# A second projection whose products are added up in PSUM: TensorE keeps adding into banks that have already been read

## The chip, the core and the metric

The kernel runs on one core of one Trainium2 chip. A core has five engines with a queue each: TensorE (matrix products, results only into PSUM), VectorE, ScalarE, GpSimd and SyncE, which here only starts transfers. PSUM has eight banks of 512 fp32 values per partition; one product of this kernel fills one bank. The time is that of the whole program on the device, in microseconds. Beside the timed runs there is one profiled execution, from which the profile and the trace come.

## The reference: what is computed

One layer of an encoder for 2048 tokens of width 1024 in fp32: windowed attention, then a SwiGLU feed-forward network with 2816 hidden units, each followed by a normed, gated residual:

```python
h = rmsnorm(x, ffn_norm_pre[i]) * (1.0 + sc2) + sh2
y = swiglu(h, ffn_w_in[i], ffn_w_out[i])       # (silu(a) * b) @ w_out
x = x + g2 * rmsnorm(y, ffn_norm_post[i])
```

The change lies in `@ w_out` (the second projection: 2816 values in, 1024 out) and in the norm and residual after it.

## The kernel before, in words

*How fp32 is kept.* Every fp32 factor is split into a high half, rounded to the matmul's input type by ScalarE, and a low half, the rest, by VectorE (`split`, L149 to L151). A product of two 128-wide tiles is then three matmuls: high by high, high by low, low by high.

*How the projection is tiled.* The tokens are done in two halves of 1024, each half as two chunks of 512. The output's 1024 columns are two groups of 512. So a half's result is a 2 x 2 block matrix (column group i, chunk j), and the 2816 hidden values are 11 pairs of 128-wide tiles. For each pair the 2 x 2 by 2 x 2 block product is done with seven products in place of eight, by Winograd's form of Strassen's method. The factors are sums of blocks: s1 to s4 of the weights, made by GpSimd (L1147, L1148, L1166, L1168), and t1 to t4 of the hidden values, made earlier and kept in DRAM (`g_d`). With P1 = a11 b11, P2 = a12 b21, P3 = s4 b22, P4 = a22 t4, P5 = s1 t1, P6 = s2 t2, P7 = s3 t3, the four results are

```
(0,0) = P1 + P2          (0,1) = P1 + P6 + P5 + P3
(1,0) = P1 + P6 + P7 + P4    (1,1) = P1 + P6 + P7 + P5
```

*How it is staged.* `PARTS` (L55) groups the pairs: parts of 2, 3, 3, 3 pairs in the first half and 3, 3, 3, 2 in the second; the last one (`LAST`) is done as eight plain products a block (`plain`, L1217). A stage is one of the seven products of one part, for the four 128-token blocks of a chunk in turn. `product` (L1196) takes a bank of the pool `psO` (six banks, used in rotation), adds the matmuls of the part's pairs in it (9 for three pairs), and empties it into an SBUF tile of its own for each product and block: in a half's first part ScalarE copies it (L1207), later VectorE adds it (L1209). So 7 x 4 running sums are kept. In the half's last such part the combinations above are made in SBUF from the seven sums (`SUMS`, L1109, at L1213; those into "2" and "3" by VectorE, the others by GpSimd).

*What comes with it.* `Weights.put` splits the weights of one stage, three stages ahead, and loads a part's raw weights into the buffers `raw0` to `raw2` as soon as their last use is over. `Grams.load` fetches the hidden factors two stages ahead into twelve buffers; for the first half it also splits them, for the second they lie in DRAM as halves. The first stages' factors are prepared while the first projection ends (`first_weights`, L987).

*The norm.* `finish` (L1233) handles one block and chunk: it loads the residual x1, squares the two result tiles with ScalarE, multiplies them by the gains with VectorE (L1245), forms the reciprocal root of the mean, scales, adds the residual (L1249) and stores. `ahead` (L1253) strings eight of these for the first half; one step of it is issued after every product of the second half's first part.

*The order.* Within an engine, instructions run in the order in which the program's planner has put them. It goes by program order as priority and by simulated times, so a changed instruction can move its neighbours.

Of the kernel before, what the change touches and what calls it, by code (L numbers as in the profile page):

```python
# [17 lines left out]
P = 128  # L18
# [49 lines left out]
def encoder_layer(ctx, tc, a):  # L68
# [361 lines left out]
    psF = open_pool(ctx, "psF", 2, space=PSUM)  # L430
# [136 lines left out]
    def make_row(col, dst, scratch, i):  # L567
        pg = psF.tile([P, CH], F32, tag="mm", name=f"pgrow{i}")
# [200 lines left out]
    def filling():  # L769
# [14 lines left out]
        make_row(coef[:, 1, :], g1row, yq.tile([P, CH], F32, tag="sq", name="growt0", bufs=1), 0)  # L784
# [202 lines left out]
    def first_weights():  # L987
# [14 lines left out]
        for i in range(2):  # L1002
            for k in range(m):
                t = b21p.tile([P, 2, CH], F32R, tag="b21", name=f"g0_{i}_{k}")
                sp.dma_start(f(t[:, 1]), g_d[0][k][("t1", "b21")[i]][:, 0])
# [3 lines left out]
        for i, n in enumerate(("s1", "a12", "a11")):  # L1009
            for k, src in enumerate(first_src):  # L1010
# [5 lines left out]
                elif n == "a12":  # L1016
                    pool.tensor_tensor(src["s4"], src["a12"], src["s2"], ALU.subtract)
# [70 lines left out]
    for hf in range(S // HALF):  # L1088
# [8 lines left out]
        if hf + 1 < S // HALF:  # L1097
# [3 lines left out]
    psc.close()  # L1101

# [8 lines left out]
    AGAIN = dict(zip("5216473", "1678924"))  # L1111
    PLACE = {(0, 0): "2", (0, 1): "3", (1, 0): "4", (1, 1): "5"}
# [9 lines left out]
    psO = open_pool(ctx, "psO", 6, space=PSUM)  # L1122
# [7 lines left out]
    class Weights:  # L1130
# [20 lines left out]
        def put(self, n=1):  # L1151
            for _ in range(n):
# [7 lines left out]
                for k, src in enumerate(self.src):  # L1160
# [6 lines left out]
                    elif name == "a12" and (hf, p) != LAST:  # L1167
# [27 lines left out]

    def product(hf, p, i, b):  # L1196
        m, name = PARTS[hf][p], PRODUCTS[i][2]
        ps = psO.tile([P, CH], F32, tag="p", name=f"po{hf}_{p}_{i}_{b}")
        for k in range(m):
            g, w = grams.g[hf, p, i, k][:, :, b * P:(b + 1) * P], wts.w[hf, p, i, k]  # L1200
            pe.matmul(ps, g[:, 0], w[:, 0], start=k == 0, stop=False)  # L1201
            pe.matmul(ps, g[:, 0], w[:, 1], start=False, stop=False)  # L1202
            pe.matmul(ps, g[:, 1], w[:, 0], start=False, stop=k == m - 1)  # L1203
        if p == 0:
            slot = AGAIN[name] if hf else name
            z[hf, b, name] = (zB if slot in "37" else zC if slot in "89" else zA).tile([P, CH], F32, tag=f"z{slot}", name=f"z{hf}_{b}_{name}", bufs=JB)
            act.copy(z[hf, b, name], ps)  # L1207
        else:
            dve.tensor_tensor(z[hf, b, name], ps, z[hf, b, name], ALU.add)  # L1209
        if (hf, p) in ((0, len(PARTS[0]) - 1), (1, len(PARTS[1]) - 2)):  # L1210
            for x, *y in SUMS.get(name, ()):
                y = [x] + y if len(y) == 1 else y
                (dve if x in "23" else pool).tensor_tensor(z[hf, b, x], z[hf, b, y[0]], z[hf, b, y[1]], ALU.add)  # L1213
# [3 lines left out]
    def plain(j, b):  # L1217

        hf, p = LAST
        for i in range(2):  # L1220
            ps = psO.tile([P, CH], F32, tag="p", name=f"pl{j}_{b}_{i}")
# [8 lines left out]
            y = z[hf, b, PLACE[i, j]]  # L1230
            dve.tensor_tensor(y, ps, y, ALU.add)

    def finish(hf, j, b):  # L1233
# [7 lines left out]
        ys = [z[hf, b, PLACE[i, j]] for i in range(2)]  # L1241
# [28 lines left out]
    end = iter(())  # L1270
    for hf, p in parts[:-1]:
        for i in range(len(PRODUCTS)):
            for b in range(JB):
                product(hf, p, i, b)
                next(end, None)
            wts.put()
            grams.load()
        if (hf, p) == (0, 0):
            with tc.issue_after(latest[0]):
                make_row(coef[:, 3, :], grow, yp.tile([P, CH], F32, tag="sq", name="growt1", bufs=2), 1)  # L1280
        if (hf, p) == (0, len(PARTS[0]) - 1):
            end = ahead([finish(hf, j, b) for b in range(JB) for j in range(CPH)])
# [66 lines left out]
```

## Time and profile before

| | |
|---|---|
| time, median of 3 runs | 2104.68 us (2103.5 to 2110.62) |
| profiled execution: its time, its span | 2106.09 us, 2104.3 us |
| TensorE busy | 2019.6 us, 96% of the span |
| VectorE, ScalarE, GpSimd busy | 1528.5, 1005.2, 969.4 us |
| second projection, first product to end of the plain part | 1654.4 to 2095.2 us of the span |

In the trace, `po` is the bank of a product, `z` the running sums, `wo_s` and `wo_a` split weights of a sum or a plain block, `wr` raw weights, `g` hidden factors. A window's row gives each engine's busy time and, in brackets, its instructions. Matmuls overlap: each is listed for about 0.39 us, though they start 0.227 us apart. A half is written 0 or 1 and a part by its number, so the second half's first part is part (1,0).

### The profile page before, as it was taken

The numbers are of one execution on the slowest core, as the hardware profiler recorded it, in microseconds if no ns is written. First come the engines' busy times: TensorE is split into PE (matmuls) and PEld (weight loads), VectorE is DVE, ScalarE is ACT, GpSimd is POOL, SyncE is SP. The second block draws the span as 40 slices with busy tenths as digits, with TensorE's granted clock in tenths as the row PEclk, the third lists the DMA queues.
The fourth block names the chain that finished last, engine by engine and source line by source line (L and its number), as shares of the span: only waits on it lengthen the run. The fifth ranks groups of instructions, "written<-read, shape, count | busy, mean of one in ns | idle before, by whom it ended". The sixth has DMA issues, their size and how long they took to land.

```text
span 2104.3 us, 28775 instructions
## 1 busy us (share of the span) xinstructions
PE 2019.6 (96%) x9416; PEld 1663.9 (79%) x9416; DVE 1528.5 (73%) x2621; ACT 1005.2 (48%) x2129; POOL 969.4 (46%) x934
## 2 busy tenths in 40 slices
PE   8797899999999998999999999999999999999998
PEld 6676787888888786888888887888888788877886
DVE  8376677667777668576676698777875689987667
ACT  4233577776777756333333344434333654435222
POOL 0412446543445535455665455555453242395340
PEclk9899999999999999999999999999999999999999
DMA  8689668565555675443743454534434454469763
GB/s 313 189 281 284 185 184 263 175 166 182 168 187 202 212 241 187 140 129 118 247 158 108 160 177 151 196 140 178 162 145 160 151 196 135 135 249 365 264 243 128
DMA packets 257286, 402.69 MB, mean 191 GB/s; under 512 B 84661, under 2 KB 135397, under 8 KB 255088
## 3 DMA queue, kind: packets, MB, share of 16 engines
q1 hardware_dynamic: 216592, 371.41, 52.3%
q10 hardware_dynamic: 39072, 25.18, 3.9%
q0 software_dynamic: 1472, 4.27, 0.5%
q8 instruction: 74, 1.21, 0.2%
q14 instruction: 76, 0.62, 0.1%
HBM read 267.83 MB, written 132.95 MB: 190 GB/s over the span
## 4 chain that ended last, share of the span: by engine, by line
PE 72%; DVE 10%; DMA 7%; POOL 4%; issue 3%; ACT 3%; SPq 0%; DVEq 0%; ACTq 0%; POOLq 0%
PE pc_i L147 12%; PE pc_i L145 12%; PE pc_i L146 12%; PE po L1202 4%; PE po L1203 4%; PE po L1201 4%; PE t L519 3%; PE psq L146 2%; PE psq L147 2%; PE psq L145 2%; PE s L497 2%; PE py L613 2%; PE py L614 2%; PE py L615 2%; PE o L525 2%
## 5 line engine op out<-in xcount | busy, mean ns | idle before, releaser
L146 PE MATMUL pc_i<-ht,ws_i 128*128 128x512 f32 x528 | 207.5, 393 | 1.6 <-DVE ht L151 1.6
L145 PE MATMUL pc_i<-ht,ws_i 128*128 128x512 f32 x528 | 206.5, 392 | 1.6 <-ACT ht L150 1.6
L147 PE MATMUL pc_i<-ht,ws_i 128*128 128x512 f32 x528 | 207.4, 393 | 0.0
L150 ACT CAST wa_i<-wiri 128x512 fp32r<-128x512 f32 x132 | 81.7, 620 | 212.6 <-PE pc_i L147 121.6
L506 POOL TENSOR_SCALAR pr<-pr,rs 128x288 f32<-128x288 f32 (+3 forms) x256 | 125.4, 509 | 117.7 <-DVE rs L504 108.0
L502 ACT ACTIVATE pr<-pr,nm 128x289 f32<-128x289 f32 (+3 forms) x256 | 135.3, 530 | 58.5 <-DVE nm L500 57.0
L500 DVE CUSTOM_DVE_ANT_0 pr<-s,bias,nsink 128x288 f32<-128x288 f32 (+3 forms) x256 | 124.0, 500 | 53.4 <-PE s L497 41.9
L878 POOL TENSOR_TENSOR s_i<-wiri 128x512 f32<-128x512 f32 x44 | 61.3, 1394 | 193.1 <-DMA wiri<-w_in 146.1
L151 DVE TENSOR_TENSOR ws_i<-s_i,ws_i 128x512 fp32r<-128x512 f32 x132 | 126.7, 960 | 24.1 <-ACT ws_i L150 23.9
L151 DVE TENSOR_TENSOR wa_i<-wiri,wa_i 128x512 fp32r<-128x512 f32 x132 | 125.2, 948 | 20.2 <-ACT wa_i L150 19.7
L145 PE MATMUL pc_i<-hb,wa_i 128*128 128x512 f32 x352 | 139.0, 395 | 0.5 <-DVE u_i L945 0.5
L151 DVE TENSOR_TENSOR plo<-t,phi 128x512 fp32r<-128x512 f32 x184 | 121.8, 683 | 24.1 <-ACT phi L150 24.0
L146 PE MATMUL pc_i<-hb,wa_i 128*128 128x512 f32 x352 | 138.2, 393 | 0.0
L147 PE MATMUL pc_i<-hb,wa_i 128*128 128x512 f32 x352 | 138.2, 393 | 0.0
L1201 PE MATMUL po<-wo_s,g 128*128 128x512 f32 x320 | 125.2, 395 | 5.9 <-ACT wo_s L150 5.3
L1202 PE MATMUL po<-wo_s,g 128*128 128x512 f32 x320 | 126.0, 394 | 1.8 <-DVE wo_s L151 1.8
L497 PE MATMUL s<-k,q 128*128 128x288 f32 (+4 forms) x512 | 110.4, 314 | 17.1 <-DMA k<-k_d 11.0
L1203 PE MATMUL po<-wo_s,g 128*128 128x512 f32 x320 | 125.7, 393 | 0.0
L519 PE MATMUL t<-ident,pr 128*128 128x128 f32 x736 | 116.2, 275 | 6.6 <-POOL pr L506 5.8
L146 PEld LDWEIGHTS pc_i<-ht,ws_i 128*128 128x128 f32 x528 | 99.7, 189 | 23.9 <-DVE ht L151 2.1
L145 PEld LDWEIGHTS pc_i<-ht,ws_i 128*128 128x128 f32 x528 | 99.9, 189 | 23.5 <-ACT ht L150 2.0
L150 ACT CAST ws_i<-s_i 128x512 fp32r<-128x512 f32 x132 | 81.6, 618 | 75.7 <-PE pc_i L147 71.1
(253 smaller groups left out, 6037.5 us busy)
## 6 DMA issues: line engine op xcount, KB each, us to landing
wiri<-w_in SPq DMA_DIRECT2D x88, 512.0 KB, 4.0
ada<-ada_w SPq DMA_DIRECT2D x40, 512.0 KB, 6.7
wr<-w_out SPq DMA_DIRECT2D x20, 1024.0 KB, 9.1
g<-g_d_t SPq DMA_DIRECT2D x36, 512.0 KB, 5.6
g<-g_d_b SPq DMA_DIRECT2D x35, 512.0 KB, 5.3
q<-q_d SPq DMA_DIRECT2D x16, 1024.0 KB, 6.6
wsr<-w_qkv SPq DMA_DIRECT2D x24, 512.0 KB, 4.9
g<-g_d_t SPq DMA_DIRECT2D x44, 256.0 KB, 3.2
```

The lines of the kernel that those rows point to most:

```text
L145: pe.matmul(ps, w[0], h[0], start=first, stop=False)
L146: pe.matmul(ps, w[0], h[1], start=False, stop=False)
L147: pe.matmul(ps, w[1], h[0], start=False, stop=last)
L150: act.copy(hi, src)
L151: return eng.tensor_tensor(lo, src, f(hi), ALU.subtract).ins
L497: m = pe.matmul(ps[:, :n], qs, kk[:, e, jb * P + lo:jb * P + hi], start=e == 0, stop=e == 1)
L502: act.activation(pr[:, i, lo:hi + 1], pr[:, i, lo:hi + 1], AF.Exp, bias=nm[:, i:i + 1], scale=-1.0, accum_out=rs[:, i:i + 1])
L506: pool.tensor_scalar(pr[:, i, lo:hi], pr[:, i, lo:hi], rs[:, i:i + 1], 1.0, ALU.mult, ALU.mult)
L519: pe.transpose(pt[:, i * P:(i + 1) * P], pr[:, i, jj * P:(jj + 1) * P], ident)
L1201: pe.matmul(ps, g[:, 0], w[:, 0], start=k == 0, stop=False)
L1202: pe.matmul(ps, g[:, 0], w[:, 1], start=False, stop=False)
L1203: pe.matmul(ps, g[:, 1], w[:, 0], start=False, stop=k == m - 1)
```

## The change

`PRODUCTS` gets a new order, and in place of a sum's name each product has a tag and a place. The tag names a set of four banks, one for each block: a or b. The first three products start their bank afresh (`FRESH`); the other four add their matmuls to what their bank already holds, after it has been read once: set a goes from P1 to P1 + P6, P1 + P6 + P7 and P1 + P6 + P7 + P4, set b from P5 to P5 + P3. After each product the bank's content of that time is added to the result at its place (or copied there, if it is the first for that place). Four results for each block are kept in SBUF, and `SUMS` with its additions is gone. The pool `psO` has eight banks, four in each set, where it had six; the two come from the pool `psF`, which now closes before. A part begins with a12 in place of s1, and s4 is made together with s2. The row of gains (`make_row`) takes a bank of set a. The norm of the first half begins one stage earlier, goes through the blocks of the first chunk before the second's, and takes a step after every second product. `first_weights` follows the new order.

```diff
-    PRODUCTS = (("s1", "t1", "5"), ("a12", "b21", "2"), ("a11", "b11", "1"), ("s2", "t2", "6"),
-                ("a22", "t4", "4"), ("s3", "t3", "7"), ("s4", "b22", "3"))
+    psf.close()
+    PRODUCTS = (("a12", "b21", "a", (0, 0)), ("s1", "t1", "b", (1, 1)), ("a11", "b11", "a", (0, 0)), ("s2", "t2", "a", (0, 1)),
+                ("s3", "t3", "a", (1, 1)), ("a22", "t4", "a", (1, 0)), ("s4", "b22", "b", (0, 1)))
+    FRESH = 3
-    SUMS = {"1": (("2", "1"),), "6": (("6", "1"), ("1", "6", "5")), "7": (("7", "6"), ("4", "7"), ("5", "7")),
-            "3": (("3", "1"),)}
...
-    psO = open_pool(ctx, "psO", 6, space=PSUM)
+    psO = open_pool(ctx, "psO", JB, space=PSUM)
...
                     if name == "s1":
                         pool.tensor_tensor(src["s2"], src["s1"], src["a11"], ALU.subtract)
-                    elif name == "a12" and (hf, p) != LAST:
                         pool.tensor_tensor(src["s4"], src["a12"], src["s2"], ALU.subtract)
...
+    bank = {}
     def product(hf, p, i, b):
-        m, name = PARTS[hf][p], PRODUCTS[i][2]
-        ps = psO.tile([P, CH], F32, tag="p", name=f"po{hf}_{p}_{i}_{b}")
+        m = PARTS[hf][p]
+        _, _, tag, at = PRODUCTS[i]
+        if i < FRESH:
+            bank[tag, b] = psO.tile([P, CH], F32, tag=tag, name=f"po{hf}_{p}_{i}_{b}")
+        ps = bank[tag, b]
         for k in range(m):
             g, w = grams.g[hf, p, i, k][:, :, b * P:(b + 1) * P], wts.w[hf, p, i, k]
-            pe.matmul(ps, g[:, 0], w[:, 0], start=k == 0, stop=False)
...
+            on = dict(skip_group_check=True) if i >= FRESH else {}
+            pe.matmul(ps, g[:, 0], w[:, 0], start=i < FRESH and k == 0, stop=False, **on)
...
-        if p == 0:
-            slot = AGAIN[name] if hf else name
-            z[hf, b, name] = (zB if slot in "37" else zC if slot in "89" else zA).tile([P, CH], F32, tag=f"z{slot}", name=f"z{hf}_{b}_{name}", bufs=JB)
-            act.copy(z[hf, b, name], ps)
+        if (hf, b, at) in z:
+            y = z[hf, b, at]
+            dve.tensor_tensor(y, ps, y, ALU.add)
         else:
-            dve.tensor_tensor(z[hf, b, name], ps, z[hf, b, name], ALU.add)
-        if (hf, p) in ((0, len(PARTS[0]) - 1), (1, len(PARTS[1]) - 2)):
-            for x, *y in SUMS.get(name, ()):
-                y = [x] + y if len(y) == 1 else y
-                (dve if x in "23" else pool).tensor_tensor(z[hf, b, x], z[hf, b, y[0]], z[hf, b, y[1]], ALU.add)
+            pl = (zC if at[0] else zB) if hf else zA
+            y = z[hf, b, at] = pl.tile([P, CH], F32, tag=f"z{at[0]}{at[1]}", name=f"z{hf}_{b}_{at[0]}{at[1]}", bufs=JB)
+            act.copy(y, ps)
...
-    end = iter(())
+    end, turn = iter(()), 0
     for hf, p in parts[:-1]:
         for i in range(len(PRODUCTS)):
+            if (hf, p, i) == (0, len(PARTS[0]) - 1, len(PRODUCTS) - 1):
+                end = ahead([finish(0, j, b) for j in range(CPH) for b in range(JB)])
             for b in range(JB):
                 product(hf, p, i, b)
-                next(end, None)
+                turn += 1
+                if turn % 2 == 0:
+                    next(end, None)
             wts.put()
             grams.load()
         if (hf, p) == (0, 0):
             with tc.issue_after(latest[0]):
-                make_row(coef[:, 3, :], grow, yp.tile([P, CH], F32, tag="sq", name="growt1", bufs=2), 1)
-        if (hf, p) == (0, len(PARTS[0]) - 1):
-            end = ahead([finish(hf, j, b) for b in range(JB) for j in range(CPH)])
+                make_row(coef[:, 3, :], grow, yp.tile([P, CH], F32, tag="sq", name="growt1", bufs=2), 1,
+                         psO.tile([P, CH], F32, tag="a", name="pgrow1"))
```

More of the change, by code (lines that the diff above doesn't have):

```diff
@@ L429, in encoder_layer @@
     ada_late = open_pool(com, "adal", 2)
-    psF = open_pool(ctx, "psF", 2, space=PSUM)
+    psf = ExitStack()
+    psF = open_pool(psf, "psF", 2, space=PSUM)
     psS = open_pool(att, "psS", 2, space=PSUM)
@@ L565, in fill_qkv, with make_row @@
                         nxt.halves(k)
-    def make_row(col, dst, scratch, i):
-        pg = psF.tile([P, CH], F32, tag="mm", name=f"pgrow{i}")
+    def make_row(col, dst, scratch, i, pg):
         pe.transpose(pg[:KT, :P], col, ident)
@@ L783, in filling @@
         g1row = yq.tile([P, D], F32, name="g1row")
-        make_row(coef[:, 1, :], g1row, yq.tile([P, CH], F32, tag="sq", name="growt0", bufs=1), 0)
+        make_row(coef[:, 1, :], g1row, yq.tile([P, CH], F32, tag="sq", name="growt0", bufs=1), 0,
+                 psF.tile([P, CH], F32, tag="mm", name="pgrow0"))
         yield from fillers_o()
@@ L1004, in first_weights @@
                 t = b21p.tile([P, 2, CH], F32R, tag="b21", name=f"g0_{i}_{k}")
-                sp.dma_start(f(t[:, 1]), g_d[0][k][("t1", "b21")[i]][:, 0])
+                sp.dma_start(f(t[:, 1]), g_d[0][k][("b21", "t1")[i]][:, 0])
                 split(t[:, 0], t[:, 1], f(t[:, 1]), dve)
@@ L1008, in first_weights @@
         yield
-        for i, n in enumerate(("s1", "a12", "a11")):
+        for i, n in enumerate(("a12", "s1", "a11")):
             for k, src in enumerate(first_src):
@@ L1015, in first_weights @@
                     pool.tensor_tensor(src["s2"], src["s1"], src["a11"], ALU.subtract)
-                elif n == "a12":
                     pool.tensor_tensor(src["s4"], src["a12"], src["s2"], ALU.subtract)
@@ L1194, in encoder_layer @@
     z = {}
+    bank = {}
     def product(hf, p, i, b):
[L1197 to L1198 removed]
+        m = PARTS[hf][p]
[3 more added lines that the diff above has]
+        ps = bank[tag, b]
         for k in range(m):
             g, w = grams.g[hf, p, i, k][:, :, b * P:(b + 1) * P], wts.w[hf, p, i, k]
[L1201 to L1213 removed]
+            on = dict(skip_group_check=True) if i >= FRESH else {}
+            pe.matmul(ps, g[:, 0], w[:, 0], start=i < FRESH and k == 0, stop=False, **on)
+            pe.matmul(ps, g[:, 0], w[:, 1], start=False, stop=False, **on)
+            pe.matmul(ps, g[:, 1], w[:, 0], start=False, stop=k == m - 1, **on)
+        if (hf, b, at) in z:
+            y = z[hf, b, at]
+            dve.tensor_tensor(y, ps, y, ALU.add)
+        else:
+            pl = (zC if at[0] else zB) if hf else zA
+            y = z[hf, b, at] = pl.tile([P, CH], F32, tag=f"z{at[0]}{at[1]}", name=f"z{hf}_{b}_{at[0]}{at[1]}", bufs=JB)
+            act.copy(y, ps)
     grow = zB.tile([P, D], F32, name="grow")
@@ L1220, in plain @@
         for i in range(2):
-            ps = psO.tile([P, CH], F32, tag="p", name=f"pl{j}_{b}_{i}")
+            ps = psO.tile([P, CH], F32, tag="ab"[i], name=f"pl{j}_{b}_{i}")
             m = PARTS[hf][p]
@@ L1229, in plain @@
                     pe.matmul(ps, g[:, 1], w[:, 0], start=False, stop=k == m - 1 and e == 1)
-            y = z[hf, b, PLACE[i, j]]
+            y = z[hf, b, (i, j)]
             dve.tensor_tensor(y, ps, y, ALU.add)
@@ L1240, in finish @@
         ss = yp.tile([P, 2], F32, tag="ss", name=f"ss{c}_{b}", bufs=3)
-        ys = [z[hf, b, PLACE[i, j]] for i in range(2)]
+        ys = [z[hf, b, (i, j)] for i in range(2)]
         for i in range(2):
```

2 lines of the change are left out of this document (removed).

## The prediction

> **What bounds the kernel now.** I read the page, then windows cut at the parts of the second projection, then windows of its tile `po` alone, then the chain of waits at the places that lose time. First the page:
>
> ```profile
> span 2104.3 us, 28775 instructions
> PE 2019.6 (96%) x9416; PEld 1663.9 (79%) x9416; DVE 1528.5 (73%) x2621; ACT 1005.2 (48%) x2129; POOL 969.4 (46%) x934
> ```
>
> TensorE is the bound, and the diff issues the same matmuls in the same number. It can therefore win only time in which TensorE waits inside the second projection, and it can lose there. One window for each part, the plain part and the tail:
>
> ```profile
> core 0: us, PE busy (x) PEld busy (x) DVE busy (x) ACT busy (x) POOL busy (x), PEclk, DMA share, GB/s
> 1654.44:1697.46 43.02, 40.43 (x170) 32.72 (x169) 27.19 (x35) 35.67 (x67) 13.52 (x10) 0.96 0.69 243
> 1697.46:1756.22 58.76, 57.42 (x253) 47.22 (x252) 53.97 (x68) 27.22 (x48) 25.74 (x17) 1.00 0.43 144
> 1756.22:1813.34 57.12, 57.12 (x253) 47.30 (x252) 50.88 (x71) 25.22 (x43) 18.34 (x12) 1.00 0.46 152
> 1813.34:1870.46 57.12, 57.12 (x253) 47.30 (x252) 49.29 (x72) 20.94 (x36) 27.92 (x19) 1.00 0.62 213
> 1870.46:1932.18 61.72, 58.61 (x253) 46.91 (x252) 53.27 (x89) 32.87 (x88) 41.79 (x37) 1.00 0.74 290
> 1932.18:1994.52 62.34, 59.14 (x254) 48.20 (x252) 41.54 (x52) 16.93 (x29) 25.00 (x18) 0.97 0.76 285
> 1994.52:2051.64 57.12, 57.12 (x254) 47.30 (x252) 39.41 (x56) 11.95 (x20) 24.70 (x17) 1.00 0.68 249
> 2051.64:2095.20 43.56, 43.56 (x193) 35.85 (x191) 34.65 (x74) 13.49 (x44) 5.01 (x4) 1.00 0.39 132
> 2095.20:2104.31 9.11, 0.12 (x1) 0.00 (x0) 4.37 (x10) 1.13 (x4) 0.00 (x0) 0.69 0.31 115
> ```
>
> A part of three pairs has 7 x 4 x 9 = 252 matmuls and takes 57.12 us where nothing waits: 0.2267 us a matmul, 2.04 a product, 8.16 a stage of four products. The first part has two pairs, so 57.12 x 2/3 = 38.08 (a stage 5.44). The losses are 43.02 - 38.08 = 4.94, then 1.64, 4.60 (the fifth window) and 5.22 (the sixth): 16.40 us in all. That is the most that can be won; the plain part loses nothing, and the diff only renames tiles in the tail. Which stages lose it, and one that does not (same columns, without GpSimd):
>
> ```profile
> 1665.73:1673.94 8.21, 5.62 (x25) 4.32 (x23) 0.00 (x0) 2.25 (x4) 1.00 0.72 245
> 1673.94:1681.14 7.20, 7.20 (x24) 5.79 (x25) 0.00 (x0) 1.54 (x3) 0.76 0.06 22
> 1697.46:1707.26 9.80, 8.46 (x37) 6.68 (x36) 0.00 (x0) 1.82 (x3) 1.00 0.20 58
> 1731.74:1739.90 8.16, 8.16 (x37) 6.76 (x36) 1.37 (x2) 0.00 (x0) 1.00 0.75 269
> 1886.78:1898.29 11.51, 8.92 (x37) 6.41 (x35) 0.00 (x0) 2.28 (x4) 1.00 0.07 12
> 1898.29:1907.38 9.09, 8.59 (x36) 6.79 (x37) 0.00 (x0) 3.10 (x6) 1.00 0.99 380
> 1932.18:1945.56 13.38, 10.18 (x38) 7.65 (x36) 1.97 (x3) 2.26 (x4) 0.87 0.98 385
> ```
>
> First part: 8.21 - 5.44 = 2.77 of waiting, then 1.76 at a clock of 0.76. Then 1.64 at the second part's first stage; 3.35 + 0.93 in the second half's first part; 5.22 at the first stage of the part after. What ended the first and the last of these, from the chain of waits:
>
> ```profile
> 1670.78 0.62 ACT g L150
> 1671.40 0.97 ACT z L1207 x2
> 1672.37 0.38 ACT g L150
> 1672.78 0.59 ACT z L1207
> 1673.37 0.53 ACT wo_s L150
> ...
> 1916.77 18.15 DMA wr<-w_out
> ...
> 1936.42 0.64 ACT wo_s L150
> 1937.08 1.42 DVE wo_s L151
> ```
>
> And in between, from the waits of 1870 to 1946 us, and SyncE's own:
>
> ```profile
> PEld po L1201 <- ACT z L1207: 5.2, 5, 3.0
> ACT sq L1244 <- POOL z L1213: 7.2, 1, 7.2
> ...
> SPq L1238 <- DVE z L1249: 22.1, 3, 17.7
> ```
>
> TensorE waited there for banks that ScalarE had not emptied, and ScalarE stood behind squares of the norm that waited for GpSimd's sums.
>
> **The change part by part.** Prices of one eviction and of the sums:
>
> ```profile
> L1209 DVE TENSOR_TENSOR z<-po,z x140: 674/685/694, 1709.0 to 2052.5; 128x512 f32<-128x512 f32 x140
> L1207 ACT COPY z<-po x56: 563/587/615, 1657.4 to 1938.5; 128x512 f32<-128x512 f32 x56
> ```
> ```profile
> L1213 POOL TENSOR_TENSOR z<-z,z 128x512 f32<-128x512 f32 x38 | 60.1, 1606 | 67.8 <-DVE z L1209 67.5
> L1213 DVE TENSOR_TENSOR z<-z,z 128x512 f32<-128x512 f32 x15 | 13.5, 900 | 0.6
> ```
>
> Evictions stay at 7 x 4 x 7 = 196, so accumulating saves none of them. Copies fall from 56 to 32 and adds rise from 140 to 164: ScalarE -24 x 0.587 = -14.1 us, VectorE +24 x 0.685 = +16.4. The sums go: -60.1 us on GpSimd, -13.5 on VectorE. VectorE's total moves by +3, which nothing waits for as such; what counts is where.
>
> *First part (4.53 of its 4.94).* The copies of stage two leave ScalarE: 0.97 + 0.59 = 1.56 us of the chain above. VectorE must add them instead before stage three enters the same banks, 4 x 0.685 = 2.74 in the worst order, so between 1.2 worse and 4.53 better. In that window ScalarE is the fuller engine (35.67 against 27.19 us of 43.02). I take the copies' 1.5 as **won**.
>
> *Second part's first stage (1.64).* Each part now begins with a12, which needs no GpSimd sum, where s1 did. But VectorE has eight more adds before it (5.5 us). Between 0 and 1.64; I take **1.0**.
>
> *Norm of the first half (4.60).* The sums that the squares waited for are gone, and the steps come every second product: 17 steps over 34 products, 69 us, not 35. Against it VectorE, 53.27 us busy in this window of 61.72, gets 12 adds (8.2 us) and loses the sums there and a sixth of the norm. Its loads and stores are as many, eight loads on SyncE, sixteen stores from GpSimd; a load that waits for its buffer (22.1 us above) still has gram loads queued behind it, which are fetched two stages, 16 us, ahead. I take the stall as gone but for 1.0: **3.6**, from -4.1 (a rival below) to 4.60. The Trainium skill ("SBUF — State Buffer", "Who interferes with whom") says that a VectorE instruction with two SBUF inputs contends with a GpSimd one that reads SBUF, and one with a single SBUF input does not. The trace agrees: at most 694 ns for the add from PSUM, 900 on average for L1213 beside GpSimd. By that rule the 1.0 would be gone too, and the sum 1.0 us better.
>
> *Part after it (5.22).* The weights' last tile took 18.15 us to land, among stores and loads of the norm at 385 GB/s, and was issued late behind the norm's VectorE work. Then s1 was summed, cast and split: from 1934.92 (1916.77 + 18.15) to the cast at 1936.42 is 1.5 us that a12 spares in any case. With the norm spread the transfer should start and land earlier. Between 1.5 and 5.22, I take **4.2**.
>
> *The banks.* Six rotating banks gave a bank five products until its next use. Now stages two to five of a part add into the same four banks, so an eviction has three products, 6.1 us. VectorE's queue in two stages where weights and grams are split, with GpSimd busy:
>
> ```profile
> 1731.94 0.69 DVE L1209 TENSOR_TENSOR z<-po,z 128x512 f32<-128x512 f32 x1
> ...
> 1735.93 0.68 DVE L1209 TENSOR_TENSOR z<-po,z 128x512 f32<-128x512 f32 x1
> ...
> 1739.34 3.47 DVE L151 TENSOR_TENSOR g<-g 128x512 fp32r<-128x512 f32 x2
> 1742.73 1.27 DVE L1209 TENSOR_TENSOR z<-po,z 128x512 f32<-128x512 f32 x2
> ...
> 1752.34 1.28 DVE L1209 TENSOR_TENSOR z<-po,z 128x512 f32<-128x512 f32 x2
> ...
> 1799.76 1.28 DVE L1209 TENSOR_TENSOR z<-po,z 128x512 f32<-128x512 f32 x2
> ```
>
> The stage began at 1731.74; the add at 1731.94 is still the last of the stage before, 1735.93 its own first, and the pair at 1742.73 its second and third. The second is done at 1743.42, but its bank is wanted at 1739.90 + 2.04 = 1741.94: 1.5 us of waiting. One part later the stage begins 57.12 us on, at 1788.86; the add is done at 1800.45 and wanted at 1799.06: 1.4. The third such part shows no late pair. Cost **-2.9**; 0 if the order falls well. If the later pair at 1752.34 (done 1753.03, wanted one stage after 1741.94, at 1750.10) stood in a chained stage, 2.9 in each of three parts, -8.8. A wait this short costs no clock: the 1.64 above ran at 1.00.
>
> The row of gains now borrows one of these banks, once, for a transpose and a small copy. Seven products lie between its turn and the next use of that bank, so I cost it at nothing; with that cover gone TensorE waits for a copy, at most L1207's 0.59.
>
> Sum: 1.5 + 1.0 + 3.6 + 4.2 - 2.9 = **7.4 us**. The span goes from 2104.3 to 2096.9. The profiled execution took 2106.09, 1.8 around its span and 1.4 above the median shown, so I take the change from the median: 2104.68 - 7.4 = **2097.3**.
>
> **The rivals.** *All stalls go* and the late pairs come out early: 16.4 won, 2088.3. For it: every loss has a cause that the diff touches. Against: the pairs are late by GpSimd's weight sums, which stay.
>
> *The gain is eaten.* The first two places stay as they are, the transfer of 18.15 us still ends last and only the 1.5 of the sum goes, the norm gives 3.6, the banks take 2.9: 2.2 won, 2102.5. For it: DMA at 385 GB/s, with the same bytes to move.
>
> *The norm's backlog meets fewer banks: slower.* In the second half's first part evictions and norm stand in the same queues. If they stay as late as now, a bank that has three products in place of five waits 2 x 2.04 = 4.1 us more than the 4.60 of today; with 2.9 in the first half and nothing won elsewhere that is +7.0, 2111.7. It decides where an eviction lags over 6.1 us. For it: VectorE at 86% gets 12 more adds. Against: no sums, half the pace. The Trainium skill ("Perfetto Trace Analysis", "Matmuls") speaks for this one: matmul groups should rotate through different banks so that one's evacuation overlaps the next. No run yet shows its price here.
>
> **How the numbers follow.** Forecast 0.48, all stalls go 0.12, eaten 0.25, slower 0.15. About 0.3%, 6.3 us, is what a measurement tells from no change: faster 0.60, same 0.25, slower 0.15. The range leaves out the outer half of the two ends: 2089 to 2108.
>
> **What would show it.** Right: part windows after of some 41.5, 59.3, 58.5, 57.1, 58.1, 58.1 and 57.1 us; no GpSimd or VectorE instruction on the sums' line; TensorE's waits for an eviction on VectorE of 1 to 2 us in the middle stages of two first-half parts; the weight transfers of the second half's second part landing before their stage. Wrong: a second half's first part over 61.7 us with TensorE waiting for adds (the slower rival), the first stage after it still waiting for `wr`, or first-half parts longer than 60 us.

## The result, and the profile after

The changed kernel takes 2089.72 us (median of 4 runs, 2086.54 to 2092.54); the kernel before, beside it, 2105.21 us. The ratio is 0.9921 with a 95% interval of 0.9901 to 0.9941: 15.5 us less. Forecast were 7.4 us less, 2097.3. The time lies in the range; the change of it is twice the forecast. A second measurement of both, below, gives 0.9945 (0.9926 to 0.9965), 11.4 us by the medians (2102.67 over 23 runs of the kernel before, 2091.29 over 7 of the changed one).

The first lines of the page of the changed kernel:

```profile
span 2084.7 us, 28731 instructions
PE 2011.4 (96%) x9416; PEld 1660.3 (80%) x9416; DVE 1505.5 (72%) x2629; ACT 994.7 (48%) x2105; POOL 912.5 (44%) x894
```

TensorE issues 9416 matmuls as before. GpSimd has 40 instructions less, ScalarE 24 less, VectorE 8 more. Windows of the changed kernel, one for each part, then the plain part (columns as in the prediction):

```profile
1645.58:1688.26 42.68, 41.16 (x170) 32.58 (x168) 31.48 (x46) 29.96 (x55) 13.45 (x10) 0.96 0.65 227
1688.26:1745.51 57.25, 57.25 (x255) 47.32 (x254) 54.89 (x72) 27.16 (x47) 26.20 (x17) 1.00 0.46 157
1745.51:1802.62 57.11, 57.11 (x253) 47.31 (x252) 50.42 (x71) 25.74 (x43) 18.73 (x12) 1.00 0.46 153
1802.62:1859.74 57.12, 57.12 (x253) 47.31 (x252) 48.69 (x72) 25.21 (x54) 18.14 (x12) 1.00 0.65 230
1859.74:1917.81 58.07, 57.46 (x253) 47.23 (x252) 48.43 (x92) 28.20 (x65) 25.20 (x28) 1.00 0.94 354
1917.81:1974.93 57.12, 57.12 (x253) 47.31 (x252) 36.91 (x50) 12.85 (x22) 18.69 (x13) 1.00 0.68 248
1974.93:2032.05 57.12, 57.12 (x253) 47.31 (x252) 32.15 (x49) 11.95 (x20) 0.00 (x0) 1.00 0.69 252
2032.05:2075.60 43.55, 43.55 (x193) 35.86 (x191) 32.35 (x72) 13.50 (x44) 0.00 (x0) 1.00 0.38 128
```

Four parts now run at 57.12 us, the time without a wait, and two others at 57.25 and 58.07. Against the windows of the kernel before, part (0,1) is 1.51 us shorter, (1,0) 3.65, (1,1) 5.22, the first part 0.34. From the first product to the end of the plain part it is 430.16 us where it was 440.88: 10.7 us less.

The rest of the difference between the two profiles lies before the change: the projection's first product starts at 1645.58 us, where it started at 1654.44, 8.9 us earlier. Up to the last stages of the first projection the two kernels have the same instructions in the same order on every engine. Fourteen profiles of this study start the projection between 1645.3 and 1654.4 us, two of them of the unchanged kernel, at 1654.4 and 1649.6. The kernel before and its variants (four profiles) start it at 1647.4 to 1654.4, the changed kernel and its variants (ten) at 1645.3 to 1652.3. So the start scatters by several microseconds by itself, and the reading below goes by the projection's own length.

Table of all profiles, from the starts of the `po` matmuls in the trace (us). The parts (0,2), (0,3) and (1,2) are 57.12 in all of them, but for 58.26 and 57.22 in the first two of "s1 first". The columns are the parts, the projection's length to the end of the plain part, and the projection's start.

| kernel | (0,0) | (0,1) | (1,0) | (1,1) | length | start |
|---|---|---|---|---|---|---|
| before | 43.0 | 58.8 | 61.7 | 62.3 | 440.9 | 1654.4 |
| before, again | 40.6 | 61.7 | 63.6 | 61.4 | 442.3 | 1649.6 |
| after | 42.7 | 57.3 | 58.1 | 57.1 | 430.2 | 1645.6 |
| after, again | 41.1 | 57.3 | 57.6 | 57.1 | 428.1 | 1648.5 |
| before, a12 first | 40.4 | 57.1 | 65.0 | 58.3 | 435.9 | 1647.4 |
| after, s1 first | 41.1 | 62.2 | 57.4 | 57.1 | 434.1 | 1650.2 |
| after, old pace | 41.1 | 57.3 | 57.8 | 57.1 | 428.2 | 1647.0 |
| after, sums back | 41.1 | 58.2 | 77.6 | 57.1 | 449.0 | 1651.0 |
| after, sums and pace back | 42.7 | 57.3 | 76.6 | 57.1 | 448.7 | 1652.3 |
| after, sums that only the norm waits for | 41.2 | 57.4 | 64.9 | 60.1 | 438.6 | 1648.2 |
| after, VectorE made late | 41.1 | 58.1 | 58.0 | 64.7 | 436.9 | 1647.8 |
| before, VectorE made late | 43.1 | 58.9 | 62.8 | 65.3 | 445.2 | 1648.6 |
| after, s2 earlier | 39.0 | 58.8 | 57.7 | 57.1 | 427.6 | 1645.3 |
| after, s2 earlier, look-ahead kept | 38.7 | 58.9 | 58.0 | 57.1 | 427.8 | 1649.1 |

Below, the *lag* of an eviction is the time from the end of its product's last matmul to its own end, and the *cover* of a bank is how long the lag may be before TensorE, which wants the bank again, has to wait.

### The profile page after: what moved, and what is told of

Read it like the earlier page. It is cut to its first block, busy times and chain, and to the rows that moved or that the text cites. A ratio compares the mean times of both kernels' runs of the same rounds, so it can differ in the third digit from the quotient of the medians.

```text
span 2084.7 us, 28731 instructions
## 1 busy us (share of the span) xinstructions
PE 2011.4 (96%) x9416; PEld 1660.3 (80%) x9416; DVE 1505.5 (72%) x2629; ACT 994.7 (48%) x2105; POOL 912.5 (44%) x894
## 4 chain that ended last, share of the span: by engine, by line
PE 42%; DVE 4%; DMA 1%; issue 1%; POOL 1%; ACT 1%; SPq 0%; DVEq 0%; ACTq 0%; POOLq 0%
PE pc_i L145 8%; PE pc_i L147 8%; PE pc_i L146 8%; PE po L1205 5%; PE po L1206 5%; PE po L1204 5%; DVE z L1245 1%; PE pl L1229 1%; PE pl L1227 1%; PE pl L1228 1%; DMA wiri<-w_in 0%; DVE z L1249 0%; DMA ht<-hd_d_t 0%; DVE z L1209 0%; DVE wo_s L151 0%
## 5 line engine op out<-in xcount | busy, mean ns | idle before, releaser
L1209 DVE TENSOR_TENSOR z<-po,z 128x512 f32<-128x512 f32 x164 | 110.6, 684 | 42.2 <-PE po L1206 40.4
L498 PE MATMUL s<-k,q 128*128 128x288 f32 (+4 forms) x512 | 110.0, 313 | 16.7 <-DMA k<-k_d 10.4
```

## The experiments

### Both kernels once more

No edit. The unchanged kernel against itself:

> The kernel before once more. Theory scatter: projection 440.8 us (within 1.5), its start anywhere from 1645 to 1655. Rival, upstream is part of the change: the start again at 1653 to 1656. Either: no difference in time from before.

> The changed kernel once more. Its first profile has 8.9 us of the difference ahead of the projection (first product at 1645.6 us, 1654.4 before), where both kernels issue the same instructions, and 10.7 us in it (first product to the last of the plain part: 430.0 us, 440.8 before). Theory scatter: the start of the projection varies from execution to execution whatever the kernel, so it lies anywhere from 1645 to 1655 here, and the projection again takes 430 us (within 1). Rival, upstream is part of the change: the start is again 1645 to 1647.

Measured: the unchanged kernel 2103.23 us, ratio to itself 1.0006 (0.9986 to 1.0026); the changed one 2091.29 us, ratio 0.9945 (0.9926 to 0.9965). What follows: the gain is there again, in the same three parts. The two starts, 1649.6 and 1648.5 us, are 1.1 apart, not 8.9, which speaks for scatter and against the rival. The changed kernel's projection is 2 us shorter than in its first profile (428.1), more than the 1 us expected, most of it (1.6) in the first part. The whole program's gain is 15.5 us in one measurement and 11.4 in the other; the projection's is 10.7 in one pair of profiles and 14.1 in the other.

### The order alone, and all but the order

The kernel before with a12 ahead of s1:

```diff
-    PRODUCTS = (("s1", "t1", "5"), ("a12", "b21", "2"), ...
+    PRODUCTS = (("a12", "b21", "2"), ("s1", "t1", "5"), ...
...
-                    elif name == "a12" and (hf, p) != LAST:
                         pool.tensor_tensor(src["s4"], src["a12"], src["s2"], ALU.subtract)
```

> The kernel before with a12 first in each part and s1 second, s4 made with s2; seven sums, six banks and the norm as before. Theory, the order alone frees a part's start of GpSimd's sum: the first half's second part 57.1 to 57.6 us, not 58.8 to 61.7, and the second half's second part 1 to 3 us under its 61.4 to 62.3. The second half's first part stays at 61 to 64. Rival, the order helps only together with the new banks: second part over 58.5.

Measured: 2094.0 us in one run, projection 435.9. Windows of parts (0,1), (1,0) and (1,1) of that kernel, then two of its waits in (1,0) and the stage after it:

```profile
1687.72:1744.84 57.12, 57.12 (x253) 47.30 (x252) 55.49 (x73) 28.35 (x49) 26.91 (x17) 1.00 0.43 148
1859.08:1924.12 65.04, 60.20 (x254) 48.88 (x252) 55.24 (x89) 32.85 (x88) 44.36 (x38) 0.95 0.72 285
1924.12:1982.43 58.31, 57.66 (x253) 47.22 (x252) 39.12 (x51) 16.93 (x29) 26.65 (x18) 1.00 0.77 291
```
```profile
ACT sq L1242 <- POOL z L1211: 9.0, 1, 9.0
...
PE po L1199 <- ACT z L1205: 4.8, 2, 3.9
```

The changed kernel with s1 ahead of a12, the sum s4 where it was, and all the rest of the change:

```diff
-    PRODUCTS = (("a12", "b21", "a", (0, 0)), ("s1", "t1", "b", (1, 1)), ...
+    PRODUCTS = (("s1", "t1", "b", (1, 1)), ("a12", "b21", "a", (0, 0)), ...
...
+                    elif name == "a12" and (hf, p) != LAST:
                         pool.tensor_tensor(src["s4"], src["a12"], src["s2"], ALU.subtract)
```

> The changed kernel with s1 first in each part, as before, and a12 second. Theory, the late adds did not come because the first weight of a part no longer waits for GpSimd's sum: the second and third part of the first half show adds 7 us late in stage five again and TensorE waiting 1.5 us for each, the second part's first stage loses 1.6 again, and the projection takes 434 to 435 us, not 430. Rival, the order of the weights does not matter and the planner's new order of VectorE's work is what spares the waits: 430 to 431.

Measured: 2093.32 us, ratio 0.9952 (0.9937 to 0.9967), projection 434.1. Windows of (0,1) and (0,2), and TensorE's waits in the two:

```profile
1691.32:1753.49 62.17, 59.33 (x254) 48.20 (x253) 58.43 (x73) 28.66 (x51) 28.07 (x18) 0.97 0.44 146
1753.49:1811.75 58.26, 57.70 (x253) 47.15 (x253) 51.26 (x71) 25.55 (x43) 18.36 (x12) 1.00 0.45 150
```
```profile
PE po L1207 <- DVE wo_s L151: 2.7, 1, 2.7
PE po L1206 <- DVE z L1211: 0.7, 3, 0.3
```

What follows. The order alone frees (0,1) wholly and (1,1) but for 1.2 us; it does nothing for (1,0), which takes 65.0 us, over the expected 61 to 64, and where ScalarE's square still stands 9.0 us behind a sum. All but the order frees (1,0) and (1,1), and loses 5.1 us in (0,1). So by the projection's length the order is worth 5.0 to 6.4 us (440.9 or 442.3 against 435.9) and the rest 5.7 to 7.8 (435.9 against 430.2 or 428.1); by the other run, the order 3.9 to 6.0 (434.1 against 430.2 or 428.1) and the rest 6.8 to 8.2. Each of the two variants has one profile. Either change suffices for most of (1,1).

The waits for an add on L1211 in the last fence are the late pairs of the prediction's term for the banks: with s1 first they are there, but smaller than expected: not 1.5 us for each. In (0,1) the second add of the fifth stage lags 5.84 us and TensorE does not wait for it; the 5.1 us lost there are the first stage's wait for a split. In (0,2) the fifth stage's second add lags 6.51 us, and the next product in that bank comes 0.61 us late; the part after begins 0.50 us late by an add of the last stage that lags 6.31, since with s1 first the last stage's banks are the next part's first. Part (0,2) loses 1.14 us in all.

### The pace of the norm

```diff
-                if turn % 2 == 0:
+                if turn % 1 == 0:
                     next(end, None)
```

> The changed kernel with one step of the norm after every product, as before; its beginning one stage earlier stays. Theory pace: VectorE fills up in the second half's first part, adds are over 6 us late, that part takes 61 us or more, and the part after it waits again for raw weights: projection 435 to 440 us. Rival sums: the sums were what held the norm up; without them the full pace is harmless: 430 to 432.

Measured: 2086.93 us, ratio 0.9929 (0.9905 to 0.9952); (1,0) 57.77 us, (1,1) 57.12. What follows: the theory fell. Once the sums are gone and the evictions don't stand behind squares, it makes no difference whether the norm takes a step after every product or after every second one. That the norm begins a stage earlier and takes the blocks in another order stayed in this run, and no run takes that back.

### The sums put back

A tile of zeros is added to the four results in the first half's last part, on the engines and in the numbers of the old sums: for each block five additions on GpSimd and two on VectorE. The results stay what they are.

```diff
...
+        if (hf, p) == (0, len(PARTS[0]) - 1):
+            for eng, places in SUMMED.get(i, ()):
+                for x in places:
+                    eng.tensor_tensor(z[hf, b, x], z[hf, b, x], nought, ALU.add)
...
+    SUMMED = {2: ((dve, ((0, 0),)),), 3: ((pool, ((0, 1), (0, 1))),), 4: ((pool, ((1, 1), (1, 1), (1, 1))),),
+              6: ((dve, ((0, 1),)),)}
```

> The changed kernel with the same 28 adds of zeros at the half's end, at its own pace of a step every second product. Theory, the sums held the norm up and the slow pace softens it: the second half's first part 58 to 61 us, the part after it under 58. Rival: both within 0.5 us of the changed kernel's 57.6 to 58.1 and 57.1.

The same with a step of the norm after every product:

> The changed kernel with the sums' work and the norm's pace both put back: in the first half's last part, at the places of the old sums, VectorE adds a tile of zeros to a result (8 adds) and GpSimd does so (20 adds), so the result stays what it was and the norm waits for them; the norm takes a step after every product. Theory, the sums held the norm up: the second half's first part, 57.6 to 58.1 us in the changed kernel, takes 60 to 64 us again and the part after it 58 to 62. Rival, what helped is that four results need fewer late additions and the banks are eight: both parts stay within 1 us of the changed kernel's.

Measured: 2110.76 and 2111.82 us in one run each, (1,0) 77.6 and 76.6 us. Window of (1,0) of the first and TensorE's waits in it:

```profile
1859.49:1937.09 77.60, 64.42 (x254) 51.46 (x253) 65.04 (x101) 30.39 (x77) 48.92 (x44) 0.89 0.74 270
```
```profile
PE po L1204 <- DVE z L1209: 8.0, 2, 4.3
PE po L1204 <- DVE tz L585: 5.2, 2, 3.8
```

Twenty microseconds, far more than either theory gave. But these two runs overstate: here the last eviction of a result had to wait for GpSimd's additions to the same tile, which no eviction of the kernel before did. So the experiment was made again, with each addition behind the last add of its result, where nothing but the norm waits for GpSimd:

```diff
-    SUMMED = {..., 3: ((pool, ((0, 1), (0, 1))),), 4: ((pool, ((1, 1), (1, 1), (1, 1))),), ...}
+    SUMMED = {..., 4: ((pool, ((1, 1), (1, 1))),), 5: ((pool, ((1, 0), (1, 0), (1, 0))),), ...}
```

> The changed kernel with additions of a tile of zeros at the first half's end in place of the old sums: as many on each engine (for each block five on GpSimd, two on VectorE), and now each after the last add of its result but that VectorE's on the second chunk's comes after its last add too; so only the norm has to wait for GpSimd, and no eviction has. Theory (the sums on GpSimd held up the norm, the norm on ScalarE and VectorE the evictions): (1,0) 59 to 63 us. Rival (in the two runs with sums put back it was an eviction's own wait for GpSimd that cost 19 us; the sums as such cost little once banks are emptied by VectorE): (1,0) 57.1 to 58.6, and the sums' 4.6 in the kernel before came from its copies and its order of the norm.

Measured: 2097.63 us in one run. Windows of (1,0) and (1,1), and four of the waits from 1860 to 1945 us:

```profile
1861.10:1925.96 64.86, 59.35 (x253) 48.27 (x252) 57.24 (x95) 30.80 (x83) 42.57 (x38) 0.97 0.70 256
1925.96:1986.05 60.09, 57.42 (x253) 47.25 (x252) 43.89 (x57) 13.36 (x23) 25.55 (x20) 1.00 0.79 301
```
```profile
ACT wo_s L150 <- POOL ws L1164: 12.9, 2, 8.9
...
ACT sq L1252 <- POOL z L1217: 7.5, 1, 7.5
...
PE po L1204 <- DVE z L1209: 5.5, 2, 4.9
...
PE po L1205 <- DVE wo_a L151: 2.7, 1, 2.7
```

What follows: the sums as such cost 6.8 to 7.3 us in (1,0) (64.86 against 58.07 or 57.60) and 3.0 in the part after it, more than (1,0) lost in all in the kernel before (4.6 and 6.5), and (1,0) is longer than the expected 59 to 63. ScalarE's square stands 7.5 us behind GpSimd, as in the kernel before (7.2, and 8.5 in its second profile). And GpSimd's next sums of weights are late behind them, so ScalarE waits for those too, 12.9 us in two waits. With these, evictions in the third stage of (1,0) lag 11.0 to 14.0 us, and TensorE waits 5.1 us at the fourth. The rival, that the sums cost little once VectorE empties the banks, falls.

### The cover of a bank, three products against five

Ten more adds from the bank into a scratch tile stand ahead of one eviction on VectorE, in the fourth stage of part (1,1); five in part (1,2). TensorE's order is pinned in both parts.

```diff
...
+        n = {(1, 1, 3, 0): 10, (1, 2, 3, 0): 5}.get((hf, p, i, b), 0)
+        if n:
+            idle = yp.tile([P, CH], F32, tag="sq", name=f"idle{p}", bufs=2)
+            for _ in range(n):
+                kept["dve"] = dve.tensor_tensor(idle, ps, z[hf, b, at], ALU.add).ins
```

> The changed kernel, with VectorE made late on purpose at two places: in part (1,1) ten more adds from the bank (into a scratch tile that nobody reads) ahead of the eviction of the fourth stage's first block, in part (1,2) five. TensorE's order is pinned there to the order written in the program. An add costs some 0.60 to 0.69 us in the rows so far, so the eviction should end about 7 to 8 us after its product in (1,1) and about 4 to 5 us in (1,2); the bank's next product comes three products, about 6 us, after it. Theory (the prediction's point of decision, a lag over 6.1 us, holds, only nothing in the changed kernel reaches it): (1,1) takes 1 to 2.5 us over 57.12, with TensorE waiting for a VectorE add, and (1,2) 57.12. Rival (a late eviction costs nothing because the order moves around it or the cover is larger): both 57.12 to 57.5. Second rival (the banks are tighter than reckoned, and the changed kernel is lucky): (1,2) loses over 0.5 too.

The same edit of the kernel before:

> The kernel before, with the same extra adds at the same two places and TensorE's order pinned alike. A bank has five products here, about 10 us, until its next use. Theory: no wait for these evictions at either place; (1,1) 61 to 63 as in the kernel before, by its first stage alone, and (1,2) 57.12. Rival (the banks' number does not matter): (1,1) longer by the same 1 to 2.5 us, at the stage after the extra adds, as in the changed kernel with them.

Measured: 2095.46 and 2104.62 us in one run each. The fourth stage of (1,1) and the stage after it, of the changed kernel, and the row that starts with the late eviction:

```profile
1943.63:1956.35 12.72, 8.33 (x37) 6.60 (x36) 11.49 (x18) 2.62 (x5) 3.89 (x3) 0.97 0.97 378
1956.35:1967.55 11.20, 11.20 (x37) 8.94 (x37) 4.88 (x8) 1.06 (x2) 4.05 (x4) 0.72 0.37 135
```
```profile
1955.56 1.89 DVE L1218 TENSOR_TENSOR z<-po,z 128x512 f32<-128x512 f32 x3
```

The same two stages of the kernel before, and its late eviction:

```profile
1959.63:1967.79 8.16, 8.16 (x37) 6.76 (x36) 7.38 (x12) 1.38 (x3) 0.02 (x1) 1.00 0.94 365
1967.79:1976.73 8.94, 8.49 (x37) 6.68 (x36) 8.23 (x13) 1.72 (x3) 7.16 (x6) 1.00 0.92 369
```
```profile
1971.73 0.69 DVE L1218 TENSOR_TENSOR z<-po,z 128x512 f32<-128x512 f32 x1
```

What follows. The splits of weights went in between the extra adds, so the lag became 10.4 us in the changed kernel and 10.6 in the one before, not the 7 to 8 expected. For the same lateness the changed kernel pays 4.56 us of waiting (12.72 - 8.16) and 3.04 at a lower clock (11.20 - 8.16), 7.6 in all; the kernel before pays 0.78 (8.94 - 8.16). The theory holds, with a bigger price. The profile puts the wait of 4.56 down to a cast of weights (`ACT wo_a`), but that ended at 1955.54 us, and the waiting matmul reads `wo_s`; the late add ends at 1956.25 and the matmul starts at 1956.35. Part (1,1) as a whole takes 64.7 us in the changed kernel and 65.3 in the one before, for which 61 to 63 were expected: there 7.4 us are lost in its first stage (15.60 - 8.16), where the kernel before loses time anyway, and not at the late eviction. In (1,2) five adds make a lag of 4.36 and 4.73, and both kernels keep 57.12.

The covers come out of it: the lag less the wait is 10.42 - 4.56 = 5.86 us in the changed kernel, 10.59 - 0.61 = 9.98 in the one before. They differ by 4.1, two products of 2.04. Three places elsewhere agree: 6.68 - 0.78 = 5.90 in (1,0) of the changed kernel, 6.51 - 0.61 = 5.90 with s1 first, and with the sums back 17.86 - 3.80 = 14.06 for a bank with seven products. So a bank covers 2.04 us for each product between, less 0.2.

### s2's weights split earlier

What the first part still loses is at its fourth stage. TensorE's waits and those of its weight loads from 1645 to 1690 us in the changed kernel:

```profile
PEld po L1204 <- DVE z L1209: 2.4, 3, 1.0
...
PE po L1204 <- DVE z L1209: 1.4, 2, 0.7
...
PEld po L1205 <- DVE wo_s L151: 0.4, 1, 0.4
```

They stand against adds and splits on VectorE. Here s2's weights of the first part are split among the first stages' factors, with the later ones a stage ahead of where they were:

```diff
-        for i, n in enumerate(("a12", "s1", "a11")):
+        for i, n in enumerate(("a12", "s1", "a11", "s2")):
...
-            self.at, self.n, self.src, self.w = 3, len(first_w), first_src, first_w
+            self.at, self.n, self.src, self.w = 4, len(first_w), first_src, first_w
```

> The changed kernel with the weights s2 of the first part split while the first projection still runs, into two buffers that are free then, as those of its first three stages are. Theory, the first part's loss is ScalarE and VectorE coming late to s2's split behind the grams: it takes 38 to 39.5 us, not 41.1 to 42.7, and the projection 425 to 427. Rival, the grams' transfer is what stage three waits for: 41 again.

The same, with the first call of `put` left out, so that the look-ahead stays at three stages:

```diff
-            wts.put()
+            if (hf, p, i) != (0, 0, 0):
+                wts.put()
```

> The changed kernel with the split of s2's weights for the first part made among the first stages' factors, before the projection begins, and with the look-ahead of the later ones unchanged at three stages (the run before this had four). Theory: the wait of the first part's fourth stage for s2's low half goes ((0,0) 39 to 40 in place of 41 to 42.7) and (0,1) stays at 57.1 to 57.6; the projection takes 425.5 to 427 us in place of 428 to 430. Rival: VectorE's work is only moved, and (0,1) or the first stages lose the same 1.6 again, projection 427.5 to 430. The time of the whole program: 1 to 3 us below the changed kernel's by the theory, 0 by the rival; against the kernel before a ratio of about 0.993.

Measured: 2088.85 us, ratio 0.9938 (0.992 to 0.9956), and 2086.34 us, ratio 0.9926 (0.9907 to 0.9946). Windows of (0,0) and (0,1) of the second, and what its weight loads waited for in (0,1):

```profile
1649.09:1687.78 38.69, 38.69 (x171) 31.27 (x169) 28.44 (x41) 27.99 (x51) 9.48 (x7) 1.00 0.73 257
1687.78:1746.70 58.92, 57.52 (x255) 47.33 (x253) 55.80 (x74) 28.32 (x49) 30.82 (x20) 1.00 0.45 154
```
```profile
PEld po L1205 <- DVE wo_s L151: 1.8, 1, 1.8
```

What follows: the first part's wait is VectorE's queue, and it goes, to within 0.6 of the 38.08 without a wait. But 1.5 to 1.7 us more are lost at the second part's second stage, for the split of s1's weights: as the rival has it, the wait has largely moved, and the projections, 427.6 and 427.8, can't be told from the 428.1 of the changed kernel's second profile. Neither variant can be called better than the changed kernel; their intervals overlap its own.

## Why the prediction was right or wrong, point by point

**The bound, and where time can be won: right.** All of the projection's gain lies in the four places that the windows showed, and the plain part and the tail did not move.

**The banks (-2.9): wrong, and the step that failed.** It cost nothing in the parts (0,1) and (0,2), where the prediction had put it. (In the first part TensorE waits 1.4 us for adds at the fourth stage, but the split of s2's weights ends last there, and with that split moved the waits for adds go too.) The prediction took the late pairs of the fifth stage, which lag 7.42 us in the profile shown there, to stay as late, because "the pairs are late by GpSimd's weight sums, which stay". The sums stay in number, but not in place. In the kernel before ScalarE stood behind them in that stretch (ScalarE's waits from 1730 to 1760 us):

```profile
ACT wo_s L150 <- POOL ws L1147: 8.6, 3, 5.1
```

In the answering stretch of the changed kernel, 1718 to 1748 us, ScalarE waits for no sum. GpSimd begins the sums at the same point of the part in both kernels, about 1 us into the fifth stage. But with a12 first the plain weights of a12 are split there, which need no sum, and the split of s1 comes a stage later. What VectorE then does in that stage:

```profile
1727.06 2.38 DVE L151 TENSOR_TENSOR g<-g 128x512 fp32r<-128x512 f32 x3
1729.37 1.28 DVE L1209 TENSOR_TENSOR z<-po,z 128x512 f32<-128x512 f32 x2
```

Three splits of grams take 2.4 us where two took 3.47. In the kernel before GpSimd is at its sums throughout those 3.47 us; here it idles for 1.1 of the 2.4, waiting for raw weights. The pair's first is out 4.78 us after its matmuls, 1.1 inside the cover of 5.9. The order's effect on this was missed: it was weighed only for a part's first stage. Two runs separate it: with a12 first the kernel before has lags of at most 4.2 in that stage, with s1 first the changed kernel has 5.8 and 6.5 and pays for the latter. Over all fourteen profiles that pair lags 5.15 to 7.42 us in (0,1) and (0,2) with s1 first (eight cases) and 3.46 to 5.63 with a12 first (twenty), always inside the cover.

So the lag was no fixed size either. In the second profile of the kernel before the same pair of (0,1) lags 5.47 us, and that of (0,2) 5.15, which three products cover:

```profile
1736.36 1.27 DVE L1209 TENSOR_TENSOR z<-po,z 128x512 f32<-128x512 f32 x2
```

The cover in the prediction was sound (6.1 was assumed, 5.9 found). The lag was read from one profile, and the order that made it late was taken to stay; with s1 first the term is 1.1 us, not 2.9, and with a12 first nothing. Why the lag differs between profiles of one kernel stays open.

The term had a second fault, on the favourable side. Only the three stages that follow one another in set a have three products between. A part's first stage has seven until set a is entered again, its second nineteen, its last two seven. There the changed kernel's longest lags lie. In (0,1) TensorE does s1's first block ahead of a12's; its bank has nineteen products, and its eviction lags 10.33 us, 12.05 in the run with VectorE late. In the last run of s2's weights a12's first block of (0,1), with seven, lags 11.69, more than the 9.98 that five products cover and less than the 14.06 of seven. And the last stage of (0,3) lags up to 8.67 in the changed kernel, which three would not have covered. TensorE waits at none of these banks.

**First part (1.5): not shown.** 43.0 and 40.6 us before, 42.7 and 41.1 after: nothing beyond the scatter. The copies are gone from the chain, as the prediction had it, but VectorE's adds and splits take their place; the first stages wait for its queue, as the last two runs show. The value lay between the bounds given and was chosen too high.

**Second part's first stage (1.0): right, too small.** 1.5 to 4.4 us, and the order alone does it.

**Norm of the first half (3.6): right in size, half right in reason.** 3.65 and 6.0 us. The sums hold the norm and the evictions up, as the run shows in which only the norm waits for them; the pace, which the prediction gave as a second reason, is worth nothing. What the norm's earlier start is worth was not tested. What is left of the stall is one add:

```profile
PEld po L1204 <- DVE tz L585: 1.0, 1, 1.0
...
PE po L1204 <- DVE tz L585: 0.6, 1, 0.6
```

These are the waits of TensorE's loads and matmuls from 1858 to 1920 us of the changed kernel. They are put down to a step of the norm, `tz`, beside the third stage's first add, which lags 6.68 us against a cover of 5.90. This is the prediction's slower rival in small, at its point of decision. At full size it is in the run with sums that only the norm waits for: (1,0) loses 7.74 us (64.86 - 57.12), where the rival's price for that part was 4.60 + 4.1 = 8.7. Its place and that price were about right. The program still takes 2097.6 us there, against 2102.5 for the kernel before beside it, as the other parts keep most of their gain; 2111 us come only where an eviction itself waits for GpSimd. What kept the rival off is that the sums left.

**Part after it (4.2): right.** 5.2 and 4.2 us: no wait is left. SyncE's rows of the last raw weights in the changed kernel:

```profile
1888.31 2.31 SPq L1139 DMA_DIRECT2D wr<-w_out  x2
...
1893.94 0.38 SPq L1139 DMA_DIRECT2D wr<-w_out  x1
```

The last is issued 23.9 us ahead of the part (1917.81 - 1893.94); before, it was issued 15.4 us ahead and took 18.15.

**VectorE's total (+3): wrong, on the favourable side.** Over the eight windows VectorE's busy time falls from 350.2 to 335.3 us. The adds rise and the sums go as reckoned, but the same splits are some 11 us shorter together. Those that take longest on average, in the projection of the kernel before and of the changed one:

```profile
L151 DVE TENSOR_TENSOR wo_s<-ws,wo_s 128x512 fp32r<-128x512 f32 x38 | 41.1, 1096 | 18.3 <-ACT wo_s L150 17.8
L151 DVE TENSOR_TENSOR wo_s<-ws,wo_s 128x512 fp32r<-128x512 f32 x38 | 31.9, 861 | 2.4 <-ACT wo_s L150 2.4
```

With the order alone they take 971 ns on average, with all but the order 999. GpSimd's sums, gone or in another place, are a likely reason; no run shows it alone.

**The sum.** Forecast 7.4 in the projection, found 10.7: of the 3.3 between them the banks give 2.9, (1,1) 1.0 and (0,1) 0.5, and the first part takes 1.15 back. The other 4.8 of the measured 15.5 us is not found in the projection. The scatter of its start is large enough for it, and the second measurement, 11.4, lies within the projection's 10.7 to 14.1. That it is chance is likely, but not shown by a run. Without it the change is one and a half times the forecast, not twice.

**The rivals.** *All stalls go* gave 2088.3, near the time, but by luck: its 16.4 us are not what the projection won, as 3.0 to 4.6 us remain in the first part and 0.5 to 1.0 in (1,0). *The gain is eaten* had the first part as it came; it fell at the second part's first stage, at the transfer, which no longer ends last, and at the banks.

## What to carry to other kernels

When banks are read and added to again, work out the cover for each stage (products until the next use, less a little) and set it against the lag of the eviction in that stage of the trace; an average number of banks says nothing. A lag read from the old kernel holds for the new one only if what makes it late keeps its place in the order, so ask of each late instruction what it stood behind, and whether the change moves that. One profile's lag is one sample: the pair that lagged 7.4 us in one profile lagged 5.5 in the next of the same kernel. A gain that is under one per cent is best read from the changed stretch itself, since the stretch ahead of it can scatter by as much.

## What the runs showed of the hardware

*The clock after a wait.* TensorE's rows in the second profile of the kernel before, at the second part's first stage:

```profile
1697.93 0.50 PE L1202 MATMUL po<-wo_s,g 128*128 128x512 f32 x1 [2.62 <-DVE wo_s L151]
...
1698.50 0.39 PE L1202 MATMUL po<-wo_s,g 128*128 128x512 f32 x1
...
1699.06 0.63 PE L1202 MATMUL po<-wo_s,g 128*128 128x512 f32 x1
```

And in the run with sums that only the norm waits for, at the first stage of (1,1):

```profile
1930.38 0.50 PE L1205 MATMUL po<-wo_a,g 128*128 128x512 f32 x1 [2.67 <-DVE wo_a L151]
1930.72 0.40 PE L1206 MATMUL po<-wo_a,g 128*128 128x512 f32 x1
...
1931.88 0.39 PE L1205 MATMUL po<-wo_a,g 128*128 128x512 f32 x1
```

After 2.62 us without a matmul the clock falls, 1.1 us after work has begun again, to matmuls of 0.63 us; after 2.67 us it does not. The granted clock in the traces shows what decides. In every one of the fourteen profiles the stretches at half clock last 3.41 us or a multiple of it (but for the one in which the program ends), and their starts lie whole multiples of 3.41 us apart: with the sums back 1878.04, 1888.28 and 1905.35 us, which is 3 and 5 times 3.413. So time falls into fixed stretches of 3.41 us, and what counts in these traces is how long TensorE is busy in one of them. Two such stretches and the next of each, first around a wait of 2.07 us in the second profile of the kernel before, then around the wait of 2.67:

```profile
1930.94:1934.35 3.41, 1.34 (x7) 0.79 (x6) 1.68 (x2) 2.57 (x6) 3.33 (x3) 1.00 1.02 407
1934.35:1937.76 3.41, 3.26 (x9) 2.05 (x8) 3.41 (x4) 2.07 (x5) 2.70 (x3) 0.50 1.04 416
```
```profile
1928.58:1931.99 3.41, 1.60 (x7) 1.35 (x8) 3.41 (x5) 0.55 (x2) 1.15 (x2) 1.00 1.04 423
1931.99:1935.40 3.41, 3.41 (x17) 2.83 (x16) 3.41 (x5) 0.00 (x0) 1.83 (x2) 1.00 1.01 408
```

The shorter wait lies whole within one stretch and costs clock; the longer one is divided between two and does not. In the projections of the fourteen profiles every stretch at full clock with TensorE idle for 1.96 us or more was followed by one at half clock, and none with 1.87 or less was, but for two in the first part, each with several short waits in it (1.5 us idle). No wait up to 1.77 us that stood alone lost clock, and every one over 2.7 did; between them it goes either way. A fall costs 1.4 to 1.6 us for one stretch and 2.2 to 2.9 for two, so a wait that is a little too long costs a third to two thirds as much again, as in the run where VectorE was made late: 4.56 us of waiting and 3.04 at a clock of 0.72. The Trainium skill ("TensorE: Matmul & The Clock Gate", Part 1) has the clock fall after an idle window of some 3.4 us that runs freely. The length of the window and that it runs freely agree with the 3.41 us here; that the window must be idle does not, since some 2 us of its 3.4 were enough.

*Banks.* The Trainium skill ("Perfetto Trace Analysis", "Matmuls") asks that matmul groups rotate through different banks so that emptying one lies beside the next. The pair of runs with VectorE made late puts a price on it: 7.6 us with three products of cover, 0.8 with five. In the changed kernel as it stands the price is the 0.78 us of (1,0).
